# Conformer convolution: the 16 shifted copies of a channel pair made by DMA from SBUF to SBUF, with two later weight loads issued ahead of them

## The chip, the cores and the metric

The kernel runs on one core of a Trainium2 chip. The metric is the device time in microseconds (us) of one execution; a comparison is made between medians of several runs of each kernel on the same chip. TensorE is called PE below, VectorE DVE, ScalarE ACT, GpSimd POOL, and SyncE SP; SP is the engine that issues every DMA of this kernel.

## The reference

Four layers over 256 positions of width 1024. Layer i has a token mixer, i mod 3: 0 is a Conformer convolution, 1 a differential attention, 2 a chunked gMLP. Each is followed by a gated feed-forward block with a short convolution of its own. So the convolution module runs twice, in layers 0 and 3, and it is the only part that the change touches:

```python
def conformer_conv(x, w_in, b_in, w_dw, b_dw, ln_g, ln_b, w_out, b_out):
    h = x @ w_in + b_in
    a, g = jnp.split(h, 2, axis=-1)
    h = a * jax.nn.sigmoid(g)
    h = causal_dwconv(h, w_dw, b_dw)          # 31 taps per channel, over positions
    h = jax.nn.silu(layer_norm(h, ln_g, ln_b))
    return h @ w_out + b_out
```

After each module: x = layer_norm(ALPHA * x + y), with everything in float32.

## The kernel before

Channels lie on partitions, 128 at a time, and positions along the free axis. The module is `conv(j, ...)`, with j = 0 for layer 0 and j = 1 for layer 3. It treats the 1024 channels as four pairs of 128-channel blocks, pr = 0 to 3, in three steps for each pair.

`project(pr)` multiplies x by the pair's two weight tiles (1 MB each, gate and value half), and leaves the result in two PSUM banks, one for each block n of the pair. For pr over 0 a weight is first split into a high and a low part (`halves`: `whi` on ACT, `wlo` on DVE), and three matmuls stand for one product. `conv_weights` issues the loads into the tile `raw`, which has four buffers; a load waits until the buffer that it takes has been read.

`glu(pr, bks)` applies bias, sigmoid (ACT, tile `sg`) and product (DVE, line 430) and writes the pair to `hp` (named `chp` in the rows: 128 partitions, 2 blocks, 30 columns of zero padding and 256 positions). Then it fills `h4`. PE computes a part of the 31 taps as matmuls whose contraction runs over 32 channels and 4 neighbouring taps at once, so it needs each group r of 32 channels in all four groups s of 32 partitions, shifted by s positions. That is 16 copies of 32 partitions for a pair, made on ACT (line 422) and DVE (line 424) in proportions that the table ACT_COPIES gives. For pr under 3 a copy covers both blocks (512 columns); for pr = 3 there is a set of copies for each block, straight after its product, so 32 of 256 columns.

`rest(pr, hp)` computes the remaining taps on ACT (line 446) and DVE (line 448) into `cv`; `taps(pr, ...)` computes the others on PE (line 461, small matmuls with the diagonal weights `dg`) and adds them to `cv` on DVE (line 464). `to_tokens` transposes `cv` on PE (line 469) into the accumulators `tm`, over which the layer norm is taken; `turn_z` transposes back (line 483), `activate` applies the SiLU on ACT (line 490), and `proj_rows` multiplies by the output weights, four loads of 1 MB (`a_w_out`), each split by `halves` as well.

PE's order is the order of the code. That of the other engines is made by a scheduler when the program is built, and each of them then works its list strictly in order. SP's list holds all DMAs of the program; a DMA whose wait isn't met holds back all behind it. A DMA signals its landing on one of eight semaphores, DMAHW0 to DMAHW7, that are taken in turn, and where a DMA takes the semaphore of the eighth before it, SP waits until that one has landed.

Of the kernel before, what the change touches and what calls it, by code (L numbers as in the profile page):

```python
# [9 lines left out]
F32 = mybir.dt.float32  # L10
F32R = mybir.dt.float32r
BF16 = mybir.dt.bfloat16
AF = mybir.ActivationFunctionType
ALU = mybir.AluOpType
AX = mybir.AxisListType

P = 128
D = 1024
T = 256
# [5 lines left out]
PAD = KW - 1  # L25
# [2 lines left out]
ALPHA = (2 * DEPTH) ** 0.25  # L28
EPS = 1e-5


GROUPS = ((6, 6, 7, 7), (6, 6, 6, 7))
ACT_COPIES = ((11, 16, 12, 9), (7, 15, 13, 8))
GMIN, GMAX = min(map(min, GROUPS)), max(map(max, GROUPS))


# [1 line left out]
def trunk(ctx: ExitStack, tc: tile.TileContext, ins, out):  # L38
    nc = tc.nc
    pe, dve, act, pool = nc.tensor, nc.vector, nc.scalar, nc.gpsimd  # L40
# [16 lines left out]
    def bank():  # L57
        return mmp.tile([P, 512], F32, name="mm", tag="mm")

    def acc_bank(t, h):  # L60
        return accp.tile([P, 512], F32, name=f"acc{t}{h}", tag=f"acc{t}{h}")

    def accs():
        return [[acc_bank(t, h) for h in range(2)] for t in range(2)]
# [4 lines left out]
    def load(src, a, b, parts=1):  # L69
        raw = wpool.tile([P, a, b], F32, name="raw", tag="raw")  # L70
        for i in range(parts):
            ks = slice(i * a // parts, (i + 1) * a // parts)
            nc.sync.dma_start(out=raw[:, ks, :], in_=src[:, ks, :])
        return raw

    def halves(raw, a, b, parts=1):
        hi = wpool.tile([P, 2048 // b, b], F32R, name="whi", tag="whi")[:, 0:a, :]
        lo = wpool.tile([P, 2048 // b, b], F32R, name="wlo", tag="wlo")[:, 0:a, :]
        with ExitStack() as st:
            for ins_ in order.values():  # L80
                st.enter_context(tc.issue_after(ins_))
            for i in range(parts):
                if parts == 1:
                    r, h, l = raw, hi, lo
                else:
                    r, h, l = [x.rearrange("p a b -> p (a b)")[:, i * (a * b // parts):(i + 1) * (a * b // parts)] for x in (raw, hi, lo)]
                act.activation(out=h, in_=r, func=AF.Identity)  # L87
                dve.tensor_tensor(out=l, in0=r, in1=h.bitcast(F32), op=ALU.subtract)  # L88
        return hi, lo

    def cols(w, c0, n=256, k0=0, kn=KT):
        return w[k0 * P:(k0 + kn) * P, c0:c0 + n].rearrange("(k p) n -> p k n", p=P)
# [119 lines left out]
    def proj_cols(ps, ws, n):  # L212

        wh, wl = ws
        for k in range(KT):
            mm3(ps[:, :T], wh[:, k, n * P:(n + 1) * P], wl[:, k, n * P:(n + 1) * P],
                xT_h[:, :, k, :], xT_l[:, :, k, :], k == 0, k == KT - 1)
# [142 lines left out]
    def conv_weights(j, pr, parts=1):  # L360
        return [load(cols(ins["a_w_in"][j], s * D + pr * 256), KT, 256, parts) for s in (1, 0)]

    def conv(j, prm, lv, turn, nxt, w_first):


        with tc.tile_pool(name=f"conv{j}", bufs=2) as p:
# [4 lines left out]
            def project(pr, ws=None):  # L371

                parts = 4 if pr == 1 and j == 0 else 1
                ws = ws or conv_weights(j, pr, parts)
                bks = [bank() for n in range(2)]
                if pr:
                    ws = [halves(w, KT, 256, parts) for w in ws]
                    for n in range(2):
                        for s in range(2):
                            proj_cols(bks[n][:, s * T:(s + 1) * T], ws[s], n)  # L380
                    return bks
                for t in range(2):
                    for n, s in ((0, 0), (1, 0), (0, 1)) if t == 0 else ((0, 0), (0, 1), (1, 0)):
                        if (t, n, s) == (1, 1, 0) and j == 0:
                            first["prm"] = prm(acc_bank(1, 1))
                        proj_cols_f32(bks[n][:, s * T:(s + 1) * T], ws[s], n, t, turn if (t, n, s) == (0, 0, 1) else None)
                    if j == 0:
                        proj_cols_f32(bks[1][:, T:], ws[1], 1, t)
                if j:
                    proj_cols(bks[1][:, T:], halves(ws[1][:, :, P:], KT, P), 0)  # L390
                return bks

            b0 = project(0, w_first)
            prm = first.get("prm") if j == 0 else prm
            b_in, b_dw, lg, lb = prm[:, 0:16], prm[:, 16:24], prm[:, 24:32], prm[:, 32:40]
# [4 lines left out]
            def diagonals(pr):  # L400
                shape = [P, 8, GROUPS[j][pr], 32]
                dg = p.tile([P, 8, GMAX, 32], F32, name="dg", tag="dg")[:, :, 0:GROUPS[j][pr], :]
                with tc.issue_after(order["dve"]):
                    dve.tensor_tensor(out=dg, in0=ident4.unsqueeze(1).unsqueeze(1).broadcast_to(shape),
                                      in1=w_pe[:, 8 * pr:8 * pr + 8, 0:GROUPS[j][pr]].unsqueeze(3).broadcast_to(shape), op=ALU.mult)
                return dg

            def glu(pr, bks):

                hp = p.tile([P, 2, PAD + T], F32, name="chp", tag="chp", bufs=3)  # L410
                pool.memset(hp[:, :, 0:PAD], 0.0)
                h4 = p.tile([P, 2, 4, PAD + T], F32, name="h4", tag="h4")
                pool.memset(h4[:, :, :, 0:PAD], 0.0)
                last = {}

                def copies(a, b):
                    for r in range(4):
                        for s in range(4):
                            src, dst = hp[32 * r:32 * r + 32, a:b, PAD:], h4[32 * s:32 * s + 32, a:b, r, PAD - s:PAD - s + T]
                            i = 4 * r + s  # L420
                            if i * ACT_COPIES[j][pr] // 16 != (i + 1) * ACT_COPIES[j][pr] // 16:
                                last["act"] = act.activation(out=dst, in_=src, func=AF.Identity).ins  # L422
                            else:
                                last["dve"] = dve.tensor_copy(dst, src).ins

                for n in range(2):
                    c = 2 * pr + n
                    sg = p.tile([P, T], F32, name="sg", tag="sg")
                    act.activation(out=sg, in_=bks[n][:, :T], func=AF.Sigmoid, bias=b_in[:, 8 + c:9 + c])
                    dve.scalar_tensor_tensor(out=hp[:, n, PAD:], in0=bks[n][:, T:], scalar=b_in[:, c:c + 1], in1=sg, op0=ALU.add, op1=ALU.mult)  # L430
                    if pr == 3:
                        copies(n, n + 1)
                if pr < 3:
                    copies(0, 2)
                return hp, h4, last

            def rest(pr, hp):

# [12 lines left out]
            def taps(pr, t0=0, t1=T, ns=(0, 1)):  # L451
                if (pr, t0) not in sums:
                    sums[pr, t0] = bank().rearrange("p (n t) -> p n t", n=2)
                ps = sums[pr, t0][:, :, 0:t1 - t0]
                for n in ns:
                    for g in reversed(range(GROUPS[j][pr])):

                        first_g = g == GROUPS[j][pr] - 1
                        a = t0 if first_g else max(t0, PAD - 4 * g - 3)
                        for r in range(4):  # L460
                            pe.matmul(out=ps[32 * r:32 * r + 32, n, a - t0:], lhsT=dg[pr][:, 4 * n + r, g, :], rhs=h4[pr][:, n, r, 4 * g + a:4 * g + t1],  # L461
                                      start=first_g, stop=g == 0)
                y = cv[pr][:, ns[0]:ns[-1] + 1, t0:t1]
                dve.tensor_tensor(out=y, in0=ps[:, ns[0]:ns[-1] + 1, :], in1=y, op=ALU.add)
# [26 lines left out]
                sl = (slice(None), t, slice(4 * q, 4 * q + 4))  # L491
                order["dve"] = split(hh[sl], hl[sl], sw).ins

            hp, h4 = [None] * 4, [None] * 4
            dg, cv, sums = [None] * 4, [None] * 4, {}

            dg[0] = diagonals(0)
            hp[0], h4[0], _ = glu(0, b0)
            cv[0] = rest(0, hp[0])
            b = project(1)  # L500
            tm = accs()
            dg[1] = diagonals(1)
            hp[1], h4[1], _ = glu(1, b)
            cv[1] = rest(1, hp[1])
            taps(0)
            b = project(2)
            for t in range(2):
                to_tokens(0, t)
            lv = lv()
            nxt = nxt()  # L510
            dg[2] = diagonals(2)
            hp[2], h4[2], _ = glu(2, b)
            taps(1)
            b = project(3)
            for t in range(2):
                to_tokens(1, t)
            dg[3] = diagonals(3)
            ws = [unit_rows(wout, 2 * q) for q in range(2)]
            hp[3], h4[3], last = glu(3, b)
            order.update(last)  # L520
            cv[2] = rest(2, hp[2])
            cv[3] = rest(3, hp[3])
# [347 lines left out]
    for i in range(DEPTH):  # L870
# [14 lines left out]
        last = i == DEPTH - 1  # L885
# [29 lines left out]
```

## Time and profile before

| | |
|---|---|
| median of 3 runs | 1334.67 us (1334.4 to 1335.15) |
| the profiled execution | 1335.99 us, its span 1334.0 us, so 2.0 us lie outside the span |
| PE busy | 1300.0 us, 97% of the span |
| DVE, ACT, POOL busy | 1030.7, 773.8 and 55.9 us |
| mean granted TensorE clock | 0.994 of full speed |
| DMA | 239.81 MB, 180 GB/s over the span |

The span is the time from the first to the last instruction of that execution. An engine's busy time counts its instructions, not what they wait for; in a timeline, a number in square brackets is the time that the engine stood idle before the row, with what ended it. The granted clock is a share of full speed, with 1.00 for 2.4 GHz and 0.50 for 1.2 GHz.

### The profile page before, as it was taken

To read this page: it belongs to the slowest core of one execution; us is meant where nothing else is said; L and a number is where in the kernel's file an instruction comes from. 1 tells how busy PE (TensorE), PEld (TensorE's weight loads), DVE (VectorE), ACT (ScalarE), POOL (GpSimd) and SP (SyncE) were. 2 spreads that over 40 slices of the span, in tenths; PEclk is the share of its full clock that TensorE was granted. 3 is DMA by queue.
4 is the path that set the end of the run, shared out by engine and by line. 5 is a ranking of instruction groups with operands and counts; after the bars stand their busy time and mean duration, and the time that the engine had idled before them with its cause. 6 is when DMAs were issued, how large, how long until landed. Compare 5 with 4: busy or idle time off the path is not lost.

```text
span 1334.0 us, 21564 instructions
## 1 busy us (share of the span) xinstructions
PE 1300.0 (97%) x8530; PEld 1123.9 (84%) x8530; DVE 1030.7 (77%) x1515; ACT 773.8 (58%) x1114; POOL 55.9 (4%) x251
## 2 busy tenths in 40 slices
PE   8979999999999999999999999999999989999997
PEld 8868888886997988886789998988888977988886
DVE  4868987777686987776779555997777986987776
ACT  4973766653674766662554442676662873666661
POOL 0000000001011000100000000000000000000000
PEclk9989999999999999999999999999999999999999
DMA  7713855553732765553967553665553731665540
GB/s 233 263 63 110 289 193 186 188 187 104 247 119 81 259 202 190 191 190 119 318 217 262 161 193 126 213 219 189 186 190 95 238 127 65 217 213 192 189 136 32
DMA packets 167938, 239.81 MB, mean 180 GB/s; under 512 B 7253, under 2 KB 135838, under 8 KB 167838
## 3 DMA queue, kind: packets, MB, share of 16 engines
q1 hardware_dynamic: 167838, 238.44, 53.8%
q8 instruction: 67, 1.10, 0.3%
q14 instruction: 33, 0.27, 0.1%
HBM read 237.38 MB, written 1.05 MB: 179 GB/s over the span
## 4 chain that ended last, share of the span: by engine, by line
PE 89%; DVE 4%; ACT 3%; DMA 1%; issue 1%; SPq 1%; POOL 0%; DVEq 0%; ACTq 0%; POOLq 0%
PE mm L224 22%; PE mm L225 11%; PE acc L107 9%; PE acc L105 9%; PE acc L106 9%; PE mm L107 6%; PE mm L105 6%; PE mm L106 6%; PE mm L232 4%; PE mm L461 2%; ACT h L422 2%; PE mm L242 2%; PE mm L820 1%; DVE cv L448 1%; PE acc L642 1%
## 5 line engine op out<-in xcount | busy, mean ns | idle before, releaser
L88 DVE TENSOR_TENSOR wlo<-raw,whi 128x2048 fp32r<-128x2048 f32 (+2 forms) x239 | 450.2, 1892 | 132.5 <-ACT whi L87 132.0
L87 ACT ACTIVATE whi<-raw 128x2048 fp32r<-128x2048 f32 (+2 forms) x239 | 377.3, 1593 | 159.4 <-PE mm L224 68.2
L224 PE MATMUL mm<-xT_s,whi 128*128 128x512 f32 x1280 | 448.0, 394 | 0.0
L225 PE MATMUL mm<-xT_s,wlo 128*128 128x256 f32 x1280 | 358.4, 280 | 0.0
L224 PEld LDWEIGHTS mm<-xT_s,whi 128*128 128x128 f32 x1280 | 239.9, 187 | 55.3
L225 PEld LDWEIGHTS mm<-xT_s,wlo 128*128 128x128 f32 x1280 | 241.7, 189 | 1.3
L286 DVE SCALAR_TENSOR_TENSOR y<-hp,prm,y 128x256 f32<-128x256 f32 x352 | 164.8, 480 | 32.3 <-ACT y L281 28.4
L281 ACT ACTIVATE y<-hp,prm 128x256 f32<-128x256 f32 x160 | 94.2, 594 | 111.0 <-DVE hp L280 110.2
L105 PE MATMUL mm<-xT_s,whi 128*128 128x256 f32 x552 | 158.5, 287 | 0.0
L107 PE MATMUL mm<-xT_s,wlo 128*128 128x256 f32 x552 | 156.2, 283 | 0.0
L106 PE MATMUL mm<-xT_s,whi 128*128 128x256 f32 x552 | 156.1, 283 | 0.0
L105 PE MATMUL acc<-whi,hh 128*128 128x512 f32 x352 | 139.6, 397 | 0.0
L107 PE MATMUL acc<-whi,hl 128*128 128x512 f32 x352 | 139.5, 396 | 0.0
L106 PE MATMUL acc<-wlo,hh 128*128 128x512 f32 x352 | 139.2, 395 | 0.0
L105 PEld LDWEIGHTS mm<-xT_s,whi 128*128 128x128 f32 x552 | 105.8, 192 | 1.9 <-issue 1.5
L106 PEld LDWEIGHTS mm<-xT_s,whi 128*128 128x128 f32 x552 | 105.8, 192 | 0.4
L107 PEld LDWEIGHTS mm<-xT_s,wlo 128*128 128x128 f32 x552 | 105.8, 192 | 0.0
L279 ACT ACTIVATE hp<-mm,prm 128x256 f32<-128x256 f32 x160 | 74.0, 464 | 13.6 <-PE mm L225 13.5
L107 PEld LDWEIGHTS acc<-whi,hl 128*128 128x128 f32 x352 | 66.1, 188 | 17.3 <-DVE hl L102 1.5
L105 PEld LDWEIGHTS acc<-whi,hh 128*128 128x128 f32 x352 | 66.1, 188 | 15.8
L106 PEld LDWEIGHTS acc<-wlo,hh 128*128 128x128 f32 x352 | 66.2, 188 | 14.1
L232 PE MATMUL mm<-xT,raw 128*128 128x128 f32 x608 | 72.7, 281 | 1.4 <-DMA raw<-in_a_w_in_dram 1.4
(160 smaller groups left out, 1649.6 us busy)
## 6 DMA issues: line engine op xcount, KB each, us to landing
raw<-in_f_w_up_dram SPq DMA_DIRECT2D x88, 1024.0 KB
raw<-in_f_w_down_dram SPq DMA_DIRECT2D x44, 1024.0 KB
raw<-in_c_w_in_dram SPq DMA_DIRECT2D x24, 1024.0 KB
raw<-in_a_w_in_dram SPq DMA_DIRECT2D x12, 1024.0 KB
raw<-in_b_w_qkv_dram SPq DMA_DIRECT2D x12, 1024.0 KB
raw<-in_c_w_out_dram SPq DMA_DIRECT2D x12, 1024.0 KB
raw<-in_a_w_out_dram SPq DMA_DIRECT2D x8, 1024.0 KB
raw<-in_b_w_o_dram SPq DMA_DIRECT2D x4, 1024.0 KB
```

The costliest lines, as they stand in the source:

```text
L87: act.activation(out=h, in_=r, func=AF.Identity)
L88: dve.tensor_tensor(out=l, in0=r, in1=h.bitcast(F32), op=ALU.subtract)
L105: pe.matmul(out=ps, lhsT=lh, rhs=rh, start=start, stop=False)
L106: pe.matmul(out=ps, lhsT=lh, rhs=rl, start=False, stop=False)
L107: pe.matmul(out=ps, lhsT=ll, rhs=rh, start=False, stop=stop)
L224: pe.matmul(out=ps, lhsT=wh[:, k, n * P:(n + 1) * P], rhs=xT_hl[:, :, k, :], start=k == 0, stop=False)
L225: pe.matmul(out=ps[:, :T], lhsT=wl[:, k, n * P:(n + 1) * P], rhs=xT_h[:, :, k, :], start=False, stop=k == KT - 1)
L232: pe.matmul(out=ps[:, t * P:(t + 1) * P], lhsT=w[:, k, n * P:(n + 1) * P], rhs=xT[:, t, k, :], start=k == 0, stop=k == KT - 1)
L242: pe.matmul(out=ps, lhsT=xT[:, t, k, :], rhs=ws[k // 4][:, k % 4, :], start=k == 0, stop=k == KT - 1)
L279: act.activation(out=hp[:, 2:], in_=ps[:, T:], func=AF.Identity, bias=b_up[:, c:c + 1])
L281: act.activation(out=yy, in_=hp[:, 2:].rearrange("p (t n) -> p t n", t=2), func=AF.Identity, scale=w2[:, c:c + 1], bias=b_dw[:, c:c + 1])
L286: dve.scalar_tensor_tensor(out=yy, in0=hp[:, d:d + T].rearrange("p (t n) -> p t n", t=2), scalar=w_[:, c:c + 1], in1=yy, op0=ALU.mult, op1 ...
```

## The change

In `glu` the copies on ACT and DVE go, with the table that divided them. SP issues 16 DMAs for a pair instead, each of them 32 partitions by up to 572 columns, with the padding and both blocks in one run of each row (2,288 bytes or a little less); pair 3 has 16 too, after both blocks. `h4` is laid out with r ahead of n for that, and its padding is no longer set by POOL, since it comes with the copies. The four loads of the weights of pairs 2 and 3 are asked for ahead of `glu(1)`. The instruction after which the later splits of weights may be issued is now the sigmoid (ACT) and the product (DVE) of `glu(3)`.

```diff
                 hp = p.tile([P, 2, PAD + T], F32, name="chp", tag="chp", bufs=3)
                 pool.memset(hp[:, :, 0:PAD], 0.0)
-                h4 = p.tile([P, 2, 4, PAD + T], F32, name="h4", tag="h4")
-                pool.memset(h4[:, :, :, 0:PAD], 0.0)
-                last = {}
-
-                def copies(a, b):
-                    for r in range(4):
-                        for s in range(4):
-                            src, dst = hp[32 * r:32 * r + 32, a:b, PAD:], h4[32 * s:32 * s + 32, a:b, r, PAD - s:PAD - s + T]
-                            i = 4 * r + s
-                            if i * ACT_COPIES[j][pr] // 16 != (i + 1) * ACT_COPIES[j][pr] // 16:
-                                last["act"] = act.activation(out=dst, in_=src, func=AF.Identity).ins
-                            else:
-                                last["dve"] = dve.tensor_copy(dst, src).ins
-
+                h4 = p.tile([P, 4, 2, PAD + T], F32, name="h4", tag="h4")
                 for n in range(2):
...
-                    if pr == 3:
-                        copies(n, n + 1)
-                if pr < 3:
-                    copies(0, 2)
-                return hp, h4, last
+                src, dst = hp.rearrange("p n t -> p (n t)"), h4.rearrange("p r n t -> p r (n t)")
+                for r in range(4):
+                    for s in range(4):
+                        nc.sync.dma_start(out=dst[32 * s:32 * s + 32, r, 0:2 * (PAD + T) - s], in_=src[32 * r:32 * r + 32, s:])
+                return hp, h4
...
             b = project(1)
             tm = accs()
+            w_in = [conv_weights(j, q) for q in (2, 3)]
             dg[1] = diagonals(1)
...
-            b = project(2)
+            b = project(2, w_in[0])
...
-            b = project(3)
+            b = project(3, w_in[1])
```

PE's list is the same instruction for instruction. SP's list in layer 0, from the load of the first weights of pair 2 on, with the semaphores that each DMA waits for. `raw` are weights, `h_231` is `h4` of pair 0, `nb`, `lng` and `lnb` are vectors spread over the partitions, and `prow` are small parameter rows. Before:

```order
L73 DMA raw<-in_a_w_in_dram 128x8x256 [waits DMAHW6_49,DMAHW5_49,DMAHW7_49,DMAHW4_49,DVE_49]
L111 DMA nb<-in_a_b_out_dram 128x1024
L73 DMA raw<-in_a_w_in_dram 128x8x256 [waits PE_49]
L111 DMA lng<-in_ln_mix_g_dram 128x1024
L111 DMA lnb<-in_ln_mix_b_dram 128x1024 [waits DMAHW0_49]
L122 DMA prow<-in_f_b_up_dram 44x128 [waits DMAHW1_49]
L122 DMA prow<-in_f_b_dw_dram 44x128 [waits DMAHW2_49]
```

and now:

```order
L71 DMA raw<-in_a_w_in_dram 128x8x256 [waits DMAHW6_49,DMAHW5_49,DMAHW7_49,DMAHW4_49,DVE_49]
L71 DMA raw<-in_a_w_in_dram 128x8x256 [waits PE_49] x2
L419 DMA h_231<-chp 32x572 [waits DVE_49,Pool_49]
L419 DMA h_231<-chp 32x571 [waits DMAHW0_49]
L419 DMA h_231<-chp 32x570 [waits DMAHW1_49]
L419 DMA h_231<-chp 32x569 [waits DMAHW2_49]
L419 DMA h_231<-chp 32x572 [waits DMAHW3_49]
L419 DMA h_231<-chp 32x571 [waits DMAHW4_49]
L419 DMA h_231<-chp 32x570 [waits DMAHW5_49]
L419 DMA h_231<-chp 32x569 [waits DMAHW6_49]
L419 DMA h_231<-chp 32x572 [waits DMAHW7_49]
```

Three weight loads of 1 MB now stand directly ahead of the 16 DMAs of pair 0, the vectors and rows have gone behind those of pair 1, and from the second DMA of the 16 on each waits for the landing of the eighth before it (the eighth of them, on DMAHW6, for the third of the weight loads).

The second place is ACT's list at the end of the convolution of layer 0, where `sg` is the sigmoid of `glu(3)`, `whi` the split of output weights and `sw` the SiLU. Before:

```order
L446 ACTIVATE cv<-chp,cprm 128x256
L429 ACTIVATE sg<-mm,cprm 128x256
L422 ACTIVATE h_837<-chp 32x256 x9
L446 ACTIVATE cv<-chp,cprm 128x256
L429 ACTIVATE sg<-mm,cprm 128x256
L422 ACTIVATE h_837<-chp 32x256 x9
L446 ACTIVATE cv<-chp,cprm 128x256
L87 ACTIVATE whi<-raw 128x2048 x2
L490 ACT_TABLE_LOAD
L490 ACTIVATE sw<-mm,cprm 128x128 x5
```

and now:

```order
L414 ACTIVATE sg<-mm,cprm 128x256
L431 ACTIVATE cv<-chp,cprm 128x256
L414 ACTIVATE sg<-mm,cprm 128x256
L431 ACTIVATE cv<-chp,cprm 128x256
L85 ACTIVATE whi<-raw 128x2048 x4
L475 ACT_TABLE_LOAD
L475 ACTIVATE sw<-mm,cprm 128x128 x5
```

The 18 copies are gone, and all four splits of the output weights stand behind the sigmoids and ahead of the SiLU, instead of two. On SP the loads for the first two of them stand ahead of the 16 DMAs of pair 3, those for the last two behind.

## Rows read from the trace of the kernel before

**Rows 1.** The page, its part on busy time: us, share, instructions.

```profile
PE 1300.0 (97%) x8530; PEld 1123.9 (84%) x8530; DVE 1030.7 (77%) x1515; ACT 773.8 (58%) x1114; POOL 55.9 (4%) x251
```

**Rows 2.** Groups by line, ACT and DVE: the copies; busy us, mean ns, idle before.

```profile
L422 ACT ACTIVATE h<-chp 32x512 f32<-32x512 f32 (+1 forms) x108 | 60.8, 563 | 11.6 <-DVE chp L430 10.1
...
L424 DVE COPY h<-chp 32x256 f32<-32x256 f32 (+1 forms) x52 | 17.7, 340 | 0.8
```

**Rows 3.** Timeline, PE, end of both convolutions: start us, us, instruction, [idle before <-releaser].

```profile
73.61 0.60 PE L469 MATMUL acc<-ident,cv 128*128 128x128 f32 x4
74.13 4.46 PE L461 MATMUL mm<-h,dg 128*32 128x128 f32 x168
...
85.04 0.69 PE L469 MATMUL acc<-ident,cv 128*128 128x128 f32 x2 [6.02 <-DVE cv L464]
85.66 5.82 PE L461 MATMUL mm<-h,dg 128*32 128x128 f32 x168
...
1089.40 0.60 PE L469 MATMUL acc<-ident,cv 128*128 128x128 f32 x4
1089.93 3.82 PE L461 MATMUL mm<-h,dg 128*32 128x128 f32 x144
...
1100.05 0.69 PE L469 MATMUL acc<-ident,cv 128*128 128x128 f32 x2 [5.86 <-DVE cv L464]
1100.66 6.66 PE L461 MATMUL mm<-h,dg 128*32 128x128 f32 x160
```

**Rows 4.** Timeline, ACT, end of the convolution of layer 0.

```profile
73.60 0.45 ACT L429 ACTIVATE sg<-mm,cprm 128x256 f32<-128x256 f32 x1
75.22 3.83 ACT L422 ACTIVATE h<-chp 32x256 f32<-32x256 f32 x9 [1.17 <-DVE chp L430]
...
79.56 0.45 ACT L429 ACTIVATE sg<-mm,cprm 128x256 f32<-128x256 f32 x1
...
85.52 3.69 ACT L87 ACTIVATE whi<-raw 128x2048 fp32r<-128x2048 f32 x2
89.23 1.28 ACT L490 ACT_TABLE_LOAD   x1
95.32 1.85 ACT L490 ACTIVATE sw<-mm,cprm 128x128 f32<-128x128 f32 x5 [4.80 <-PE mm L483]
```

**Rows 5.** Timeline, DVE, the same place.

```profile
80.61 0.48 DVE L430 SCALAR_TENSOR_TENSOR chp<-mm,cprm,sg 128x256 f32<-128x256 f32 x1
81.13 2.07 DVE L424 COPY h<-chp 32x256 f32<-32x256 f32 x7
```

**Rows 6.** Windows: width, busy us of PE, PEld, DVE, ACT, POOL, granted clock, DMA share, GB/s.

```profile
80.00:82.00 2.00, 0.00 (x0) 0.00 (x0) 1.90 (x6) 0.85 (x4) 0.00 (x0) 0.92 0.16 46
```

**Rows 7.** Timeline, PE, the taps of pair 0 in layer 0.

```profile
39.86 5.05 PE L461 MATMUL mm<-h,dg 128*32 128x256 f32 x90 [1.22 <-ACT h L422]
```

**Rows 8.** Timeline, SP: issues of DMAs; start us, us, line, count.

```profile
0.81 0.86 SPq L858 DMA_DIRECT2D xa<-in_x_dram  x2
...
12.36 3.51 SPq L350 DMA_DIRECT2D prow<-in_a_w_dw_dram  x7
...
79.61 1.08 SPq L122 DMA_DIRECT2D prow<-in_f_w_dw_dram  x3
...
312.45 0.43 SPq L111 DMA_DIRECT2D lk<-in_b_lk_dram  x1
...
1032.98 0.35 SPq L111 DMA_DIRECT2D lng<-in_ln_mix_g_dram  x1
```

**Rows 9.** Windows again: the weight loads of layer 0, and 1 us after an issue.

```profile
26.00:36.00 10.00, 10.00 (x86) 10.00 (x85) 9.86 (x16) 9.06 (x13) 0.00 (x0) 1.00 1.01 339
...
1033.80:1034.20 0.40, 0.40 (x6) 0.40 (x5) 0.40 (x1) 0.00 (x0) 0.00 (x0) 1.00 0.40 154
```

**Rows 10.** Timelines, PE and DVE: the first users of two loads.

```profile
3.59 1.09 PE L161 MATMUL mm<-ident,xa 128*128 128x128 f32 x4 [3.59 <-DMA xa<-in_x_dram]
...
317.30 0.23 DVE L593 TENSOR_TENSOR lq<-lq,lk 128x64 f32<-128x64 f32 x1 [0.24 <-DMA lk<-in_b_lk_dram]
```

More of the change, by code (lines that the diff above doesn't have):

```diff
@@ L32 @@
 GROUPS = ((6, 6, 7, 7), (6, 6, 6, 7))
-ACT_COPIES = ((11, 16, 12, 9), (7, 15, 13, 8))
 GMIN, GMAX = min(map(min, GROUPS)), max(map(max, GROUPS))
@@ L428, in glu @@
                     sg = p.tile([P, T], F32, name="sg", tag="sg")
-                    act.activation(out=sg, in_=bks[n][:, :T], func=AF.Sigmoid, bias=b_in[:, 8 + c:9 + c])
-                    dve.scalar_tensor_tensor(out=hp[:, n, PAD:], in0=bks[n][:, T:], scalar=b_in[:, c:c + 1], in1=sg, op0=ALU.add, op1=ALU.mult)
-                    if pr == 3:
-                        copies(n, n + 1)
-                if pr < 3:
-                    copies(0, 2)
-                return hp, h4, last
+                    last["act"] = act.activation(out=sg, in_=bks[n][:, :T], func=AF.Sigmoid, bias=b_in[:, 8 + c:9 + c]).ins
+                    last["dve"] = dve.scalar_tensor_tensor(out=hp[:, n, PAD:], in0=bks[n][:, T:], scalar=b_in[:, c:c + 1], in1=sg, op0=ALU.add, op1=ALU.mult).ins
+                src, dst = hp.rearrange("p n t -> p (n t)"), h4.rearrange("p r n t -> p r (n t)")
[3 more added lines that the diff above has]
+                return hp, h4
             def rest(pr, hp):
@@ L460, in taps @@
                         for r in range(4):
-                            pe.matmul(out=ps[32 * r:32 * r + 32, n, a - t0:], lhsT=dg[pr][:, 4 * n + r, g, :], rhs=h4[pr][:, n, r, 4 * g + a:4 * g + t1],
+                            pe.matmul(out=ps[32 * r:32 * r + 32, n, a - t0:], lhsT=dg[pr][:, 4 * n + r, g, :], rhs=h4[pr][:, r, n, 4 * g + a:4 * g + t1],
                                       start=first_g, stop=g == 0)
@@ L492, in activate @@
                 order["dve"] = split(hh[sl], hl[sl], sw).ins
-            hp, h4 = [None] * 4, [None] * 4
+            hp, h4, last = [None] * 4, [None] * 4, {}
             dg, cv, sums = [None] * 4, [None] * 4, {}
             dg[0] = diagonals(0)
-            hp[0], h4[0], _ = glu(0, b0)
+            hp[0], h4[0] = glu(0, b0)
             cv[0] = rest(0, hp[0])
@@ L501, in conv @@
             tm = accs()
+            w_in = [conv_weights(j, q) for q in (2, 3)]
             dg[1] = diagonals(1)
-            hp[1], h4[1], _ = glu(1, b)
+            hp[1], h4[1] = glu(1, b)
             cv[1] = rest(1, hp[1])
             taps(0)
-            b = project(2)
+            b = project(2, w_in[0])
             for t in range(2):
@@ L511, in conv @@
             dg[2] = diagonals(2)
-            hp[2], h4[2], _ = glu(2, b)
+            hp[2], h4[2] = glu(2, b)
             taps(1)
-            b = project(3)
+            b = project(3, w_in[1])
             for t in range(2):
@@ L518, in conv @@
             ws = [unit_rows(wout, 2 * q) for q in range(2)]
-            hp[3], h4[3], last = glu(3, b)
+            hp[3], h4[3] = glu(3, b)
             order.update(last)
```

## The prediction

> **What bounds the kernel now.** I read the page's busy times first: PE works in 97% of the span [rows 1], and its list of instructions is not changed, so only the time in which PE stands, or runs at the lower clock, can be won. The table of waits and then PE's timeline show where that is in the two convolutions. The largest stops of the whole program are the two ahead of the transposes of pair 2, 6.02 us in layer 0 and 5.86 us in layer 3, both ended by the addition on line 464 on DVE [rows 3]. The timelines of ACT and DVE tell why that addition is late. The last product of pair 3 waits for a sigmoid that ACT begins at 79.56, because nine copies of the block before stand ahead of it from 75.22 on [rows 4]; the product comes at 80.61, seven copies follow on DVE from 81.13 for 2.07 us, and then the addition [rows 5]. PE has nothing left at 79.02 (85.04 less 6.02). The third stop is at the first taps of layer 0, where PE waits 1.22 us for a copy on ACT [rows 7]. In the window from 80 to 82 the granted clock is 0.92 [rows 6]: with levels of 1.00 and 0.50 that is 0.32 us at the lower one, so it fell at 81.68, 2.66 us after PE ran dry. The 168 small matmuls after the stop take 5.82 us where the 168 before it took 4.46, so the clock costs 1.36 us there; in layer 3 it is 6.66 us for 160 against 3.82 us for 144, or 2.42 us [rows 3].
>
> **What the change removes.** 108 copies on ACT (60.8 us) and 52 on DVE (17.7 us) [rows 2]. Nearly all of it lay beside PE's work; on the path were only the copies of pair 3, and those of pair 0. POOL's settings of the padding lay beside everything and are worth nothing.
>
> **The new chain for pair 3.** PE ends the projection at 73.61 and the sigmoid of the last block can start there; with 0.45 us for it [rows 4] and 0.48 us for the product [rows 5], and some 0.2 us of handing over, SP can issue the first of 16 DMAs at 74.75. How fast it issues: three small loads took 1.08 us, 0.36 us each, and seven in a form with one more dimension took 3.51 us, 0.50 us each [rows 8]. The 16 are of the plain form, so I take 0.38 us, near the first, and keep 0.36 and 0.50 as ends; a price below that would need SP to issue faster than any row shows. How long one takes to land isn't in the trace, since no DMA there goes from SBUF to SBUF. The lower end: an issue at 1032.98 [rows 8] moves its first bytes in the window from 1033.8 on [rows 9], so nothing lands in under 1.0 us, and I take 1.3 as the least. The upper end: a load issued at 312.45 was used at 317.30 after a wait for it, 4.85 us [rows 8, 10], though with short rows and others ahead. The nearest row is the first load of the program, alone in its queue: issued at 0.81, used at 3.59, 2.78 us for 256 KB [rows 8, 10]. At 339 GB/s [rows 9] 0.77 us of that is its bytes; 73 KB need 0.2 us, which makes 2.2, and as a read inside SBUF should not be slower than that one of a cold start I take 1.9. So the last copy of pair 3 lands at 74.75 + 15 x 0.38 + 1.9 = 82.35. The addition that PE waited for now runs well before 79.02, the transposes that it held take 0.6 us, and the taps of pair 3 start at 82.35 instead of 85.66: 3.3 us won. PE still stands for 2.7 us. In layer 3 the same steps from 1089.40 give 1098.14 instead of 1100.66 [rows 3]: 2.5 us won, with a stop of 3.35 us. Both stops last as long as the 2.66 us after which the clock fell before, so I leave the cost of the clock as it is.
>
> The Trainium skill ("DMA: Bandwidth & Descriptors", section "Anatomy of one DMA — SWDGE (gpsimd) path") gives a DMA 2.0 us plus its bytes at 436 GB/s, for another issuing engine; by it a copy would land after 2.2 us and the sum below would be 0.8 us less of a gain, which no run here shows yet.
>
> **The new chain for pair 0 in layer 0.** Here three weight loads of 1 MB stand ahead of the DMAs, which come while these still move, and the eighth DMA waits for the third load. From 26 to 36 the queue moved 339 GB/s [rows 9], so 3.15 MB end at 35.3 and the landing is known at about 36.0. The eighth is issued then, the 16th eight issues later at 39.04, and it lands at 40.94. PE then has the 5.05 us of taps that it began at 39.86 [rows 7]: 1.1 us lost. PE stands from 38.64 on, 2.3 us, less than the 2.66 us above, so I take the clock to hold. In layer 3 pair 0 has only two loads ahead of it, and by the same steps its last copy lands before PE wants it; pairs 1 and 2 have an entire projection between product and taps. They cost nothing, with that projection as cover, and would cost what their chain exceeds it by.
>
> **Loads that move.** The last two loads of output weights now come behind the 16 DMAs of pair 3, at 80.83. With 1.0 us to the first bytes, 2.1 MB at 339 GB/s and 0.7 us to the end they are there at 88.7; ACT splits the second in 1.85 us and loads its table in 1.28 [rows 4], so it is free for the SiLU at 91.8. The SiLU began at 95.32 [rows 4] and is wanted 3.3 us sooner, at 92.0. So this is just hidden, and it is the next bound: layer 0 can't win more than 3.5 us while these loads stand there. The vectors that have gone behind pair 1 are wanted only by the layer norm, tens of us later.
>
> **Sum.** With p for the pitch of issues and L for the landing, the three places give 15p + L, 15p + L and 8p + L, so each 0.1 us of pitch costs 3.8 us and each us of landing 3.0 us. At 0.38 and 1.9: -3.3 - 2.5 + 1.1 = -4.7 us. The profiled execution was 1335.99 us, 2.0 us outside its span and 1.3 us above the median of the runs; it would be 1331.3, and the median 1334.67 goes to 1330.0.
>
> **Rivals.**
> (a) The wait that replaces: pair 0's stop lowers the clock. Its stop is only 0.4 us shorter than the time to the fall, and the third load may be later. The price is the mean of the two measured, 1.9 us: -2.8, 1331.8.
> (b) The late loads hold the SiLU. For it speaks a slack of 0.2 us. If they land 2 us later, layer 0 loses 1.8 and layer 3, with 1.0 us of slack by the same bound, 1.0: 1332.8.
> (c) Bytes and not issues set the pace: 73 KB at 339 GB/s are 0.22 us. Then pair 3 is ready when PE is, no clock falls, and the late loads bound both ends at about 6.1 us each: -6.1 - 6.1 - 0.2, 1322.3. Against it: no issues of SP stand under 0.36 us apart [rows 8]. The Trainium skill speaks for it ("DMA: Bandwidth & Descriptors", section "Issuing engines are not separate DMA queues": the time to initiate a DMA is usually small against the DMA itself); the rows on SP disagree for transfers of this size.
> (d) Slower: eight semaphores for 16 DMAs. The ninth copy waits for the landing of the first. While a landing takes under 8 x 0.38 = 3.04 us nothing is seen of it. Above that the two ends pay twice, 5 us of time for each us: at 3.04 the gain is 1.3 us, at 3.3 it is gone. With 4.85 us, the upper end, it is +7.7, and 1.9 for the clock: 1344.3.
> (e) The change doesn't do what it says: something else on DVE ends the stops of pair 3, and only the loss at pair 0 stays, with the clock: +3.0, 1337.7. Against it: the nine copies on ACT stand straight ahead of the sigmoid.
>
> **How the numbers follow.** Forecast 0.43, (a) 0.20, (b) 0.10, (c) 0.08, (d) 0.12, (e) 0.07. A difference under 0.2%, 2.7 us, can't be told from none. The forecast's own spread: pitch 0.36 to 0.50 gives -0.8 to +4.6, landing 1.3 to 2.4 gives -1.8 to +1.5, the clock staying up at both ends gives up to -1.4 more by the bound of the late loads. So of its 0.43 I put 0.32 on faster and 0.11 on the same; (a) goes half to each, (b) mostly to the same, (c) to faster, (d) and (e) mostly to slower. That makes faster 0.52, same 0.29, slower 0.19. The range from 1326 to 1339 leaves out (c) and the upper part of (d).
>
> **What would show it.** In the trace after: issues of line 419 on SP 0.36 to 0.40 us apart; PE's stop in the transposes of pair 2 gone, and a stop of 2.5 to 3.5 us ended by a DMA ahead of the taps of pair 3 in both layers; the same at the first taps of layer 0, with an end at 40 to 42; the SiLU no later than ACT's table. Wrong it would be if copies land in over 3 us, if issues take 0.5 us, or if the first taps of layer 0 start after 43.

## The result and the profile after

The changed kernel takes 1354.79 us (median of 4 runs, 1352.68 to 1355.83) where the kernel before takes 1334.56: the ratio is 1.0147, 95% interval 1.0135 to 1.0158. The prediction, 1330.0, is wrong in its sign. The profiled execution has a span of 1353.2 us against 1334.0, 19.2 us more.

The page's busy times, then one row of PE's table of waits (total us, times, longest us), then the issues of line 419 on SP (ns min/median/max):

```profile
PE 1310.5 (97%) x8530; PEld 1127.2 (83%) x8530; DVE 1014.3 (75%) x1463; ACT 715.7 (53%) x1006; POOL 53.9 (4%) x243
```

```profile
PE mm L446 <- DMA h<-chp: 22.0, 14, 3.9
```

```profile
L419 SPq DMA_DIRECT2D h<-chp x128: 507/589/1471, 31.2 to 1118.1; - x128
```

PE does the same 8530 matmuls and counts as busy for 10.5 us longer, because more of them ran at the lower clock. ACT is 58 us less busy than in [rows 1]. The 11.9 us that PE waited for the addition are nearly gone (0.9 us are left), and 22.0 us of waiting for the DMA copies stand in their place. One issue takes 0.59 us, and the next begins 0.63 us after it.

PE in the two convolutions, to be held against [rows 3, 7] (start us, us, instruction, idle before; where the window that was shown ends inside a row, its time and count stop there):

```profile
38.20 0.81 PE L446 MATMUL mm<-h,dg 128*32 128x256 f32 x2 [1.89 <-DMA h<-chp]
...
44.32 4.22 PE L446 MATMUL mm<-h,dg 128*32 128x256 f32 x40 [1.45 <-DMA h<-chp]
...
80.19 0.60 PE L454 MATMUL acc<-ident,cv 128*128 128x128 f32 x4
...
86.95 0.44 PE L454 MATMUL acc<-ident,cv 128*128 128x128 f32 x2
91.25 0.60 PE L446 MATMUL mm<-h,dg 128*32 128x128 f32 x2 [3.87 <-DMA h<-chp]
...
97.75 6.47 PE L446 MATMUL mm<-h,dg 128*32 128x128 f32 x144 [2.07 <-DMA h<-chp]
...
132.67 1.03 PE L159 MATMUL mm<-ident,xa 128*128 128x128 f32 x8
...
1049.24 1.04 PE L159 MATMUL acc<-ident,xa 128*128 128x128 f32 x8
...
1072.96 4.25 PE L446 MATMUL mm<-h,dg 128*32 128x256 f32 x80 [1.48 <-DMA h<-chp]
...
1106.68 0.60 PE L454 MATMUL acc<-ident,cv 128*128 128x128 f32 x4
...
1120.25 4.99 PE L446 MATMUL mm<-h,dg 128*32 128x128 f32 x124 [1.87 <-DMA h<-chp]
...
1153.81 1.04 PE L159 MATMUL mm<-ident,xa 128*128 128x128 f32 x8
```

Three marks of the kernel before that [rows 3] does not have (transposes ahead of and behind layers 0 and 3):

```profile
119.12 1.03 PE L161 MATMUL mm<-ident,xa 128*128 128x128 f32 x8
...
1034.04 1.04 PE L161 MATMUL acc<-ident,xa 128*128 128x128 f32 x8
...
1134.94 1.03 PE L161 MATMUL mm<-ident,xa 128*128 128x128 f32 x8
```

PE's list is the same, so the same mark in both traces gives the delay up to there, and differences of delays give the places (PE came to the taps of pair 0 in layer 0 already 1.7 us sooner than in the trace of before, at 36.31 instead of 38.01; over the traces of all kernels here this mark varies from 35.1 to 38.1, with the first loads of the program, so the 1.7 us are no gain of the change, and counted from PE's arrival the place adds 6.2 us and not 4.46):

| mark on PE | before | after | delay | what it adds |
|---|---|---|---|---|
| layer 0, all taps of pair 0 can run | 39.86 | 44.32 | 4.46 | pair 0: 4.46 |
| projection of pair 3 ended | 73.61 | 80.19 | 6.58 | the low clock there: 2.12 |
| all taps of pair 3 can run | 85.66 | 97.75 | 12.09 | wait at pair 3: 5.51 |
| transposes behind layer 0 | 119.12 | 132.67 | 13.55 | mostly the low clock: 1.46 |
| transposes ahead of layer 3 | 1034.04 | 1049.24 | 15.20 | 1.65 outside the change |
| layer 3, projection of pair 3 ended | 1089.40 | 1106.68 | 17.28 | pair 0: 2.08 |
| all taps of pair 3 can run | 1100.66 | 1120.25 | 19.59 | wait at pair 3: 2.31 |
| transposes behind layer 3 | 1134.94 | 1153.81 | 18.87 | given back: -0.72 |
| span | 1334.0 | 1353.2 | 19.2 | 0.3 |

Why the copies of pair 3 come so late shows on SP's timeline (start us, us, line, count; a row of several issues includes the waits between them):

```profile
69.86 10.71 SPq L419 DMA_DIRECT2D h<-chp  x16
80.68 1.08 SPq L71 DMA_DIRECT2D raw<-in_a_w_out_dram  x2
81.86 14.16 SPq L419 DMA_DIRECT2D h<-chp  x16
...
86.18 1.26 SPq L419 DMA_DIRECT2D h<-chp  x1
90.44 0.51 SPq L419 DMA_DIRECT2D h<-chp  x1
...
95.43 0.59 SPq L419 DMA_DIRECT2D h<-chp  x1
...
1107.99 10.65 SPq L419 DMA_DIRECT2D h<-chp  x16
1118.05 0.59 SPq L419 DMA_DIRECT2D h<-chp  x1
```

In layer 3 no load holds SP at pair 3: 16 issues take 10.65 us, the last begins at 1118.05, and PE goes on at 1120.25, 2.2 us later. In layer 0 the two loads of output weights, 2 MB, were issued at 80.68, since SP had been busy until 80.57 with the DMAs of pair 2 (in the kernel before the first of the four loads was issued at 38.95 and the last at 61.87). Seven copies follow; the eighth takes the semaphore of the second load and is issued only when that has landed, at 90.44. SP's table of waits has it (total us, times, longest us):

```profile
SPq L419 <- DMA raw<-in_a_w_out_dram: 3.0, 1, 3.0
```

The last copy begins at 95.43, and PE goes on at 97.75.

The clock, by windows (width, busy us of PE, PEld, DVE, ACT, POOL, granted clock, DMA share, GB/s):

```profile
38.00:42.00 4.00, 2.00 (x5) 0.50 (x6) 4.00 (x7) 2.41 (x4) 0.00 (x0) 0.55 0.46 110
...
96.00:100.00 4.00, 2.25 (x51) 2.28 (x55) 0.00 (x0) 0.00 (x0) 0.00 (x0) 0.50 0.79 201
...
335.00:339.00 4.00, 3.83 (x5) 1.63 (x6) 2.88 (x5) 3.96 (x5) 0.00 (x0) 0.57 0.00 1
```

PE's broken work at pair 0 and at pair 3, with stops of up to 3.9 us between a few matmuls, runs at 0.55 and 0.50, and 0.50 is the level of 1.2 GHz. The 90 matmuls from 44.32 on take 7.17 us in all, where the same 90 took 5.05 [rows 7]. The third window explains the 1.65 us outside the change: PE stood 1.89 us there, as it did before (1.93 us, at 321.66), but this time the clock fell behind it. In the window from 38, with only the copies issued and the weight loads landed, the 16 DMA engines are 46% busy: the copies are not limited by what the DMA engines move.

### The profile page after: what moved, and what is told of

It is laid out like the page before. It is cut to its first block, busy times and chain, and to the rows that moved or that the text cites. A ratio compares the mean times of both kernels' runs of the same rounds, so it can differ in the third digit from the quotient of the medians.

```text
span 1353.2 us, 21606 instructions
## 1 busy us (share of the span) xinstructions
PE 1310.5 (97%) x8530; PEld 1127.2 (83%) x8530; DVE 1014.3 (75%) x1463; ACT 715.7 (53%) x1006; POOL 53.9 (4%) x243
## 4 chain that ended last, share of the span: by engine, by line
PE 91%; DMA 3%; SPq 2%; DVE 2%; issue 1%; ACT 1%; POOL 0%; DVEq 0%; ACTq 0%
PE mm L222 22%; PE mm L223 11%; PE acc L105 9%; PE acc L103 9%; PE acc L104 9%; PE mm L105 6%; PE mm L103 6%; PE mm L104 6%; PE mm L230 5%; PE mm L446 3%; SPq L419 2%; PE mm L240 2%; DMA raw<-in_a_w_in_dram 1%; PE mm L806 1%; DMA raw<-in_a_w_out_dram 1%
## 5 line engine op out<-in xcount | busy, mean ns | idle before, releaser
L446 PE MATMUL mm<-h,dg 128*32 128x128 f32 (+12 forms) x1248 | 58.8, 329 | 22.1 <-DMA h<-chp 22.0
```

## The experiments

Twelve kernels, in the order in which they ran. Theory 1 is that the number of issues sets the pace. Its rival, that of the prediction's case (c), is that bytes do; that the packets or rows of a DMA do is a third possibility.

**Half the width.** Each DMA moves the first block only; the copies of the second block are left out, and its part of `h4` is set to zero.

```diff
+pool.memset(h4[:, :, 1, :], 0.0)
...
-nc.sync.dma_start(out=dst[32 * s:32 * s + 32, r, 0:2 * (PAD + T) - s], in_=src[32 * r:32 * r + 32, s:])
+nc.sync.dma_start(out=dst[32 * s:32 * s + 32, r, 0:PAD + T], in_=src[32 * r:32 * r + 32, s:s + PAD + T])
```

> The 16 DMAs of a pair stay 16, but each moves only the first 286 of its 572 columns (36 KB instead of 73 KB; the second block's copies are left out and read as zeros). Theory 1, the number of issues sets the pace (0.63 us from one issue to the next on SP, 2.07 us to landing): the rows of SP stay 0.6 us apart and the time stays at 1354.8, within 3 us. [...] Theory 3, the bytes themselves pace at the rate of the weight loads: 1325 to 1335.

1340.0 us, ratio 1.0032 (1.0021 to 1.0042). By the time alone theory 1 is wrong, but the rows of SP say otherwise:

```profile
L420 SPq DMA_DIRECT2D h<-chp x128: 507/589/1627, 28.4 to 1101.9; - x128
...
73.53 13.12 SPq L420 DMA_DIRECT2D h<-chp  x16
```

An issue still takes 0.589 us. The edit did a second thing that the expectation had missed: these DMAs read block 0 alone, so they need not wait for the second product, and the 16 of pair 3 began while PE was still in the projection (73.53, its end is at 76.68). At pair 3 the gain is that of an earlier start. The run says nothing on bytes; a clean one follows below.

**Two issuing engines.** SP issues the DMAs with even s, ACT those with odd s.

```diff
-nc.sync.dma_start(...)
+(nc.sync, nc.scalar)[s % 2].dma_start(...)
```

> The same 16 DMAs, those with odd s issued by ACT, those with even s by SP. Theory 1, each engine's issuing sets the pace: 8 issues of 0.63 us side by side instead of 16, 5.0 us off each chain. Layer 3 then loses nothing at pair 0 and its pair 3 starts at the time that the kernel before has or sooner; layer 0 still waits for weight loads ahead of the copies at both ends. Time 1338 to 1346. Rival, the pace is set behind the engines (descriptors made or moved one after the other for both): issues on each engine come 1.2 us apart and the time stays at 1352 to 1357. Against both: ACT now spends 8 x 0.6 us per pair on issuing ahead of its splits of weights.

1344.19 us, 1.0061 (1.0040 to 1.0082), within the range of theory 1. The issues per engine, and a place in layer 3:

```profile
L419 ACTq DMA_DIRECT2D h<-chp x64: 514/602/1386, 32.3 to 1106.9; - x64
L419 SPq DMA_DIRECT2D h<-chp x64: 507/590/1268, 32.3 to 1108.4; - x64
...
1094.08 1.91 SPq L71 DMA_DIRECT2D raw<-in_f_w_up_dram  x2
1097.25 11.78 SPq L419 DMA_DIRECT2D h<-chp  x8
```

Each engine pays its own 0.6 us. In layer 3 pair 0 has no stop any more. At pair 3 there the expectation failed: two loads of the next block, 2 MB, now stand ahead of the copies, and the eight issues on SP take 11.78 us; the taps start 14.8 us after the projection instead of sooner than before. So loads ahead of the copies hold them as well, beside the number of issues.

**The weight loads back in their old place.** The DMAs stay.

```diff
-w_in = [conv_weights(j, q) for q in (2, 3)]
...
-b = project(2, w_in[0])
+b = project(2)
...
-b = project(3, w_in[1])
+b = project(3)
```

> The DMAs stay, but the weights of pairs 2 and 3 are asked for where the kernel before asked for them. If the loads ahead of the copies were the cause of the loss in layer 0 (three loads ahead of pair 0), taking them away gives 4 to 7 us back: 1348 to 1351. Theory 1 says otherwise: on SP the weights of pair 3 then stand behind the 16 DMAs of pair 2, which wait for the product of pair 2 and take 10 us, so PE waits for weights ahead of the projection of pair 3, some 15 to 20 us in each layer: 1380 to 1395.

1365.64 us, 1.0228 (1.0208 to 1.0249): slower still, though less than expected, since the wait is there in layer 0 only.

```profile
PE mm L103 <- ACT whi L85: 14.4, 1, 14.4
```

On SP the weights of pair 3 stand behind the 16 DMAs of pair 2, and PE waits 14.4 us for their split. So without the moved loads the change would have cost more; moving them is not what cost it its time. At pair 0 of layer 0 alone they cost 1.1 us: all taps can run 12.0 us after the first issue here, and 13.1 us after it in the changed kernel.

**DMAs for pairs 1 and 2 alone.** Pairs 0 and 3 are copied by ACT and DVE in the old proportions.

```diff
+by_dma = pr in (1, 2)
...
+if not by_dma:
+    copies(0, 2)
```

> DMAs for pairs 1 and 2 alone; pairs 0 and 3 are copied by ACT and DVE in the proportions of the kernel before; the moved loads stay moved. If, as the prediction held, pairs 1 and 2 cost nothing because a projection covers them: 1334.6, from 1332 to 1337 (the stops of 6 us ahead of the transposes of pair 2 stay, since pair 3 is as before). Rival: the 16 issues of pair 2 hold the loads of output weights back on SP by 10 us, which the last splits and the SiLU then wait for: 2 to 6 us more, 1337 to 1341.

1329.59 us, 0.9951 (0.9932 to 0.9970): 0.5% faster than the kernel before, and outside both expectations. ACT at pair 3, before (first row) and in this run, with PE's start of the taps of pair 3 in this run:

```profile
65.33 7.74 ACT L422 ACTIVATE h<-chp 32x512 f32<-32x512 f32 x12 [1.42 <-DVE chp L430]
```

```profile
67.20 0.47 ACT L429 ACTIVATE sg<-mm,cprm 128x256 f32<-128x256 f32 x1 [7.25 <-PE mm L106]
68.28 3.83 ACT L422 ACTIVATE h<-chp 32x256 f32<-32x256 f32 x9 [0.60 <-DVE chp L430]
...
78.48 0.73 PE L466 MATMUL mm<-h,dg 128*32 128x128 f32 x20
```

Before, twelve copies of pair 2 keep ACT until 73.07, and the first sigmoid of pair 3 comes at 73.60 [rows 4]. Here it comes at 67.20, as soon as PE has finished the first block. So the copies of pair 2 seem to have stood on the path, one pair further back than the prediction looked; the run with pair 2 alone tests it.

**No DMA at all, only the earlier loads.** The kernel of the run before, with one line changed.

```diff
+by_dma = pr in ()
```

> No DMA copies at all: ACT and DVE copy every pair in the proportions of the kernel before; of the change only the earlier weight loads and the layout of h4 stay. Both theories: nothing that PE waits for is moved by the loads, so 1334.6, from 1333 to 1336.5. If the loads alone were worth something (they land before the projections of pairs 2 and 3 in both kernels), the difference shows here, and is then to be taken off the result of pairs 1 and 2.

1333.64 us, 0.9986 (0.9977 to 0.9995): a difference of 0.14%, under the 0.2% that the prediction took as the least that can be told from none. So the earlier loads and the new layout account for about 0.14%, or 0.23% at the end of the interval, of what the runs below and above won.

**DMAs for pair 2 alone.**

```diff
+by_dma = pr in (2,)
```

> DMAs for pair 2 alone. Theory from the rows of the run with pairs 1 and 2: before, the twelve copies of pair 2 on ACT (7.74 us, from 65.33 to 73.09) held back the first sigmoid of pair 3 to 73.60, where its bank had been ready by about 67; with pair 2 off ACT and DVE this sigmoid starts at 67 to 68 and the stop of 6 us ahead of the transposes of pair 2 shrinks to 1 to 3 us, in layers 0 and 3. Then pair 2 alone gives nearly all of what pairs 1 and 2 gave: 1328.5 to 1331.5. Rival: it was the freed time of ACT and DVE in general, to which pair 1 added as much: 1331.5 to 1334.

1330.29 us, 0.9963 (0.9951 to 0.9976). The first sigmoid of pair 3 starts at 67.79, and the stop of 6.02 us ahead of the transposes has gone; PE waits 2.21 us for the DMAs of pair 2 ahead of its taps instead. Pair 2 alone has 0.37% where pairs 1 and 2 have 0.49%; the two intervals overlap.

```profile
67.79 0.47 ACT L429 ACTIVATE sg<-mm,cprm 128x256 f32<-128x256 f32 x1 [3.48 <-PE mm L106]
```

```profile
76.51 6.07 PE L466 MATMUL mm<-h,dg 128*32 128x128 f32 x162 [2.21 <-DMA h<-chp]
82.51 0.51 PE L130 MATMUL mm<-ident,prow 44*128 44x44 f32 x5
82.95 0.44 PE L474 MATMUL acc<-ident,cv 128*128 128x128 f32 x2
```

**All output weights behind the copies of pair 3.** The changed kernel with one line moved.

```diff
-ws = [unit_rows(wout, 2 * q) for q in range(2)]
 hp[3], h4[3] = glu(3, b)
 order.update(last)
+ws = [unit_rows(wout, 2 * q) for q in range(2)]
```

> The changed kernel with all four loads of output weights asked for behind the 16 DMAs of pair 3 (in the changed kernel two stand ahead of them). Theory: in layer 0 SP held the eighth copy of pair 3 from 87.44 until the second of these loads had landed, at 90.4; without them the 16 are issued at 0.63 us from 80.7 on, the last lands at 92.3 and PE starts the taps of pair 3 there instead of at 97.75; layer 3, where the two loads were issued 5.6 us before the copies, gains under 1 us. Against it stands that the splits of output weights come 5 us later. Time 1347.5 to 1351. Rival: the 16 issues alone set the end, and the loads were beside them: 1353 to 1356.

1354.43 us, 1.0141 (1.0121 to 1.0160): no gain, and the time that the rival had.

```profile
79.72 0.60 PE L454 MATMUL acc<-ident,cv 128*128 128x128 f32 x4
...
93.37 6.80 PE L446 MATMUL mm<-h,dg 128*32 128x128 f32 x156 [1.88 <-DMA h<-chp]
...
107.18 1.02 PE L468 MATMUL mm<-ident,xT 128*128 128x128 f32 x5 [3.40 <-DVE xT L463]
```

Yet the mechanism of the theory is right for the taps: all taps of pair 3 can run 13.65 us after the projection instead of 17.56 (13.57 in layer 3 of the changed kernel), so the loads held them for 3.9 us. But the splits wait for the later loads, the layer norm stands behind a split in DVE's list, and most of the gain comes back as a stop of 3.40 us ahead of the SiLU (0.79 us in the changed kernel). The time expected was wrong, since I took that price as small.

**Pairs 1 and 2 by DMA, splits behind the copies.** The run with pairs 1 and 2, with the same line moved.

> DMAs for pairs 1 and 2, ACT and DVE for 0 and 3, and the first two splits of output weights asked for behind the copies of pair 3 (in the run with pairs 1 and 2, ACT did a split of 1.91 us twice between those copies, at 76.60 and 80.26, and PE waited 1.5 and 0.66 us for the copies). Theory: the copies of pair 3 end 3.8 us sooner, PE's stops in the taps of pair 3 go, 2 to 3 us in each layer: 1323.5 to 1327. Rival: the splits that come later hold the SiLU or the first product with the output weights instead: 1328 to 1331.

1329.28 us, 0.9953 (0.9937 to 0.9968), as without the move: the rival. The copies end sooner, and a wait for an addition on DVE replaces that for them.

```profile
86.23 3.22 PE L466 MATMUL mm<-h,dg 128*32 128x128 f32 x56 [2.47 <-DVE cv L469]
```

**Half the width, cleanly.** The middle columns, which need both products; the other columns are left out and set to zero.

```diff
+pool.memset(flat[:, :, 0:143], 0.0)
+pool.memset(flat[:, :, 429:], 0.0)
...
-nc.sync.dma_start(out=dst[32 * s:32 * s + 32, r, 0:2 * (PAD + T) - s], in_=src[32 * r:32 * r + 32, s:])
+nc.sync.dma_start(out=dst[32 * s:32 * s + 32, r, 143:429], in_=src[32 * r:32 * r + 32, s + 143:s + 429])
```

> The half-width run again, without what blurred it: each of the 16 DMAs moves the middle 286 columns, which hold a part of both blocks, so that the first issue waits for both products as in the changed kernel (the other columns are left out and read as zeros). In the earlier half-width run the DMAs needed block 0 alone and could start one block sooner, and its issues still took 0.589 us each. Theory 1, an issue costs 0.63 us whatever it moves: 1353 to 1356.5, and taps of pair 3 in layer 3 start 13.3 to 13.7 us after PE's projection as in the changed kernel. Rival, bytes or packets set the pace after all: 1338 to 1346.

1355.97 us, 1.0161 (1.0146 to 1.0177): half the bytes and no time won. The issues of this run, then the page's row on the DMA queue (packets, MB, share of 16 engines) for the changed kernel and for this run:

```profile
L422 SPq DMA_DIRECT2D h<-chp x128: 507/589/1786, 33.9 to 1119.5; - x128
```

```profile
q1 hardware_dynamic: 173982, 247.80, 56.2%
```

```profile
q1 hardware_dynamic: 173982, 243.14, 54.5%
```

This settles it against bytes. It does not settle it against packets or rows: the run has as many packets as the changed kernel, 6144 more than the 167838 of the kernel before, or 48 for each of the 128 DMAs, and each DMA still has 32 rows. No run here changes the rows of a DMA. Against both speaks that the 88 loads of 1 MB of the feed-forward weights (line 71, `raw<-in_f_w_up_dram`) take 0.37 us to issue at the median in the changed kernel; they come from DRAM, so they do not decide it. The start of pair 3's taps in layer 3 was missed by 1.6 us (15.3 after the projection): in this kernel three loads, not two, stand ahead of the copies there.

**Eight DMAs and eight copies for a pair.** SP takes s of 0 and 2, ACT s = 1, DVE s = 3.

```diff
-nc.sync.dma_start(...)
+to, frm = dst[32 * s:32 * s + 32, r, 0:2 * (PAD + T) - s], src[32 * r:32 * r + 32, s:]
+if s % 2 == 0:
+    nc.sync.dma_start(out=to, in_=frm)
+elif s == 1:
+    act.activation(out=to, in_=frm, func=AF.Identity)
+else:
+    dve.tensor_copy(to, frm)
```

> Eight DMAs for a pair (s of 0 and 2), and four copies each on ACT and DVE (s of 1 and 3), whole rows of up to 572 columns. Theory 1: each chain is eight issues shorter, 5.0 us: layer 3 loses nothing at pair 0, and its last copy of pair 3 lands 13.5 - 5.0 = 8.5 us after the projection, 2.7 us sooner than the kernel before begins there; in layer 0 the eighth DMA of pair 3 is still held by the loads of output weights and that of pair 0 by the third weight load, but nothing follows behind them: 5 us less each. With two spells of low clock gone: 1330 to 1338. Rival: the waits for the landing of the eighth DMA before, which are the same for the first eight, set both ends: 1342 to 1350.

1330.83 us, 0.9970 (0.9960 to 0.9980): 24 us less than with 16, and 0.3% faster than the kernel before. So the number of DMAs is the cause, directly and by what stands behind them in SP's list: the loads of output weights are all issued by 68.0 here, 8 us ahead of the copies of pair 3, where the changed kernel had issued two of them 1.2 us ahead. The place that is left, on SP and then on PE:

```profile
76.27 5.58 SPq L421 DMA_DIRECT2D h<-chp  x8
```

```profile
81.83 1.44 PE L452 MATMUL mm<-h,dg 128*32 128x128 f32 x6 [2.80 <-DMA h<-chp]
```

**Pair 0 copied, the others by DMA.** As in the run with pairs 1 and 2, with another choice of pairs.

```diff
+by_dma = pr in (1, 2, 3)
```

> DMAs for pairs 1, 2 and 3, pair 0 copied by ACT and DVE as before. By PE's marks pair 0 cost 6.6 us in layer 0 (4.5 us of waiting and 2.1 of low clock) and 2.1 us in layer 3: 1354.8 - 8.7 = 1346, from 1344 to 1348.5, if the places add up. Rival: the time lost at pair 0 is partly only moved, since the 16 issues of pairs 1 to 3 on SP then begin sooner against loads that end at the same time: 1349 to 1352.

1342.45 us, 1.0056 (1.0040 to 1.0073): 12.3 us less than the changed kernel, where the places gave 8.7. Pair 0 cost at least what the marks say, and more through what follows it: SP's work is done sooner, and all taps of pair 3 in layer 0 can run 14.1 us after the projection (87.44 after 73.34) instead of 17.56, which is 3.5 us.

**Eight DMAs, splits behind the copies.** The loads of output weights stay where they were, and only their splits move.

```diff
-ws = [unit_rows(wout, 2 * q) for q in range(2)]
+wo = [load(...) for q in range(2)]
 hp[3], h4[3] = glu(3, b)
 order.update(last)
+ws = [halves(w, 2, D) for w in wo]
```

> Eight DMAs and eight copies for a pair as in the run before, and the splits of the first two output weights asked for behind the copies of pair 3 (their loads stay where they were). With eight DMAs, the first of pair 3 in layer 0 was issued at 76.27, 4.1 us after PE's projection ended (1.3 us in layer 3), since ACT split a weight at 71.59 and DVE its low part ahead of the last sigmoid and product. Theory: with the splits out of that chain the first issue comes 1.3 us after the projection, the last copy lands 7 x 0.63 + 2.07 = 6.5 us later, 7.8 us after the projection against the 6.9 us that PE still has work for; the stop of 2.8 us shrinks to about 1 and the spell of low clock in layer 0 goes: 1326 to 1329. Rival: something else on DVE holds the product back, or the splits that come later hold the SiLU: 1330 to 1332.

1329.24 us, 0.9960 (0.9946 to 0.9974). The first issue of pair 3 comes at 73.57, 1.6 us after the projection; the stop of 2.80 us has become three of 0.64 to 0.77.

```profile
73.57 5.86 SPq L421 DMA_DIRECT2D h<-chp  x8
```

```profile
81.06 3.20 PE L452 MATMUL mm<-h,dg 128*32 128x128 f32 x79 [0.77 <-DMA h<-chp]
```

The profiled execution lies at 1327.55, as theory had it; the median is just above its range, and a spell of low clock remains. This kernel, the two with pairs 1 and 2 and that with pair 2 lie within 1.1 us of each other, and the runs do not rank them.

## Why the prediction was wrong, point by point

- **The bound.** Right: PE's list did not change, and the whole difference is PE's stops and its clock.
- **The pitch of issues: the step that failed.** It took 0.38 us, from three small loads, with 0.50 as the upper end. Measured: 0.63 from one issue to the next. By the prediction's own rate, 3.8 us for each 0.1, that is 9.5 us: the sum of -4.7 becomes +4.8, the sign of the result. Its ends were rows of loads from DRAM, all smaller, and the upper end was treated as a bound, which those rows could not make it. Two of the three signs by which it would be wrong came: issues over 0.5 us, and taps of pair 0 of which all but six ran only after 43.
- **The rest of the gap.** Between -4.7 and the 19.2 us by which the span grew lie 24 us. Most of it has a place: beside the 9.5 us of the pitch, 3.9 are the two loads ahead of pair 3 in layer 0, 3.6 the low clock behind the stops there and at pair 0 (1.46 and 2.12), 2.1 pair 0 of layer 3, and 1.65 lie outside the change. These are readings of one execution of each kernel.
- **The landing.** Nearly right: 1.9 us forecast; 2.2 us from the start of the last issue to PE's next matmul where nothing is ahead.
- **Pair 0.** In layer 0 it forecast +1.1, and it was 4.46 at the mark and 2.12 of low clock. The third load does hold the eighth DMA, which is issued at 37.10 instead of 36.0; eight issues at the true pitch take 2.0 us more than forecast, and the landing 0.3. It took the clock to hold, since the stop would be shorter than 2.66 us. That is no fixed time: in [rows 6] the clock fell 2.66 us after PE ran dry, in layer 3 of the same trace it was still 1.00 at 1098, 3.8 us after PE ran dry at 1094.19, and in the changed kernel it fell at 38.44, 2.1 us after PE ran dry at 36.31. So rival (a)'s mechanism held too. In layer 3, where the first issue came at 1060.97 and PE at 1070.85, the forecast pitch would have had the last copy there at 1068.6; that cover of 2.3 us was less than the 3.8 us by which 15 issues were mis-sized: 2.1 us lost instead of none.
- **Pairs 1 and 2.** Forecast to cost nothing, with a projection as cover. The cover is not enough for pair 2 in layer 0: its 16 issues end at 80.57, behind the projection's end at 80.19, and PE stands 1.02 us for them; 2.21 us where pair 2 alone is moved.
- **Pair 3 in layer 0.** Forecast -3.3; measured +5.5 at the start of its taps, and +1.5 behind it. Beside the pitch a term was left out: it put the third load ahead of the eighth DMA into the sum for pair 0, and not the two loads of output weights ahead of pair 3, though the section on the change names both. The run with those loads behind puts it at 3.9 us.
- **Pair 3 in layer 3.** Forecast -2.5; measured +2.3, 4.8 us more, of which 15 x 0.25 = 3.8 us is the pitch.
- **"On the path were only the copies of pair 3, and those of pair 0."** Wrong: those of pair 2 were on it, as the run with pair 2 alone shows. The timeline of ACT had it in the eight microseconds ahead of the first row in [rows 4]: PE had finished the first block some 5.5 us before its sigmoid began (the sigmoid of the run with pairs 1 and 2 starts at 67.20, and its projection ends at 72.70). Here lay the gain that the change could have had.
- **The late loads.** Rival (b) hardly decided in the changed kernel: ACT was through with splits and table at 108.84, PE began the transposes for the SiLU at 108.14, and PE's stop behind the SiLU is 0.33 us. It did decide in the run with all of them behind, 3.4 us.
- **Rival (c)** falls by the clean half-width run. The Trainium skill ("DMA: Bandwidth & Descriptors", section "Issuing engines are not separate DMA queues") calls the time to initiate a DMA usually small against the DMA itself. Here one issue, 0.59 us, is a quarter of the 2.2 us from its start to the copy's use, and 16 of them in one list, 10.1 us, are far more than that.
- **Rival (d)**, the semaphores, was the right place with the wrong condition: what SP waits for is the landing of a load of 1 MB that has taken the same semaphore, not that of a copy.

Not shown: why an issue takes 0.59 us where other loads in these traces take 0.27 to 0.58. It is not the length of a row; the number of rows or packets, fewer partitions and other sources were not tried.

## What to carry to other kernels

Count the issues before the bytes: a small copy that becomes a DMA can cost its queue as much time as the copy cost an engine (here 0.63 us from issue to issue, against 0.63 us for a copy of both blocks on ACT), one after the other, and everything on that queue moves with it. Size a price from rows of the same form, and where there is none, let the range reach to where the verdict changes. Look for the queued work ahead of the late instruction one stage further back than the stall: moving that stage alone, most of which a projection hides, won 0.4% where moving all of it lost 1.5%.

## What the runs showed that I had not expected

- An issue of a DMA from SBUF to SBUF takes the same 0.589 us for 32 rows of 2,288 bytes and of 1,144 bytes, on ACT 0.602 us. The 0.563 us of a copy on ACT in [rows 2] is a mean over two shapes: in the trace of the kernel before a copy of both blocks on ACT took 0.63 us and one of one block 0.42 us.
- Two engines that issue together do not halve the time in full: in layer 0 eight issues each for pair 2 took 7.76 us on SP and 6.21 us on ACT, instead of 16 in 10.71 on SP alone; SP stood still twice among them, for 1.5 and 1.1 us.
- A copy behind weight loads lands with them: the four copies of pair 3 that PE's first taps need were issued in layer 0 from 81.86 on, the fourth at 84.08, and these taps started at 91.25, 7.2 us later, against 2.2 us from the start of an issue with nothing ahead.
- After stops of the same length at the same place (1.93 and 1.89 us) the clock stayed up in one execution and fell in the other, which cost 1.65 us.
